# Shifted transposes out of PSUM in 512-column operations, and weight blocks loaded one pair ahead

## The chip, the cores and the metric

One core of a Trainium2 chip runs the whole program in one launch. The time is the device time of that core in microseconds (us). The engines have queues of their own, worked in order: TensorE (PE: matmuls and transposes, results in PSUM), VectorE (DVE), ScalarE (ACT), GpSimd (POOL, which here works on SBUF only) and SyncE (SP), whose queue issues all of this kernel's loads and stores.

## The reference

Two layers of a transformer block on 1024 tokens of width 1024. Each layer has a mixer (differential attention, latent attention and a state-space scan side by side) and an MLP:

```
for l in range(DEPTH):
    mod = (cond @ w_ada[l] + b_ada[l])[:, None, :]
    sh_m, sc_m, g_m, sh_f, sc_f, g_f = jnp.split(mod, 6, axis=-1)
    h = _rmsnorm(x, norm_g[l, 0]) * (1.0 + sc_m) + sh_m
    y = _hybrid_mixer(h, ...)
    x = x + g_m * _rmsnorm(y, norm_g[l, 1])
    h = _rmsnorm(x, norm_g[l, 2]) * (1.0 + sc_f) + sh_f
    y = jnp.square(jax.nn.relu(h @ w_up[l])) @ w_down[l]
    x = x + g_f * _rmsnorm(y, norm_g[l, 3])
```

The change lies where `h` is made (the norm's result, transposed, plus the shift `sh_m` or `sh_f`) and where `h @ w_up` is computed.

## The kernel before

All matmuls work on numbers split in two: `split` makes `hi`, a rounded copy (ACT, L234), and `lo`, the rest (DVE subtraction, L235). `mm3` (L191 to L193) then runs three matmuls for each product: hi by hi, hi by lo, lo by hi.

**The next h.** Tokens are handled in eight tiles of 128. A tile of x is normed by `norm` (ACT square L629 or L631, DVE scaling L632). PE transposes it in eight blocks of 128 columns into PSUM, so that features lie on the partitions. Since the shift belongs to a feature, it is then one number per partition and block. `cut_cols` empties PSUM block by block: ACT writes `hi` with the shift as bias (L638), and DVE writes `lo` from the same block, the shift and `hi` (L639). There are three places:

- `renorm`, in the mixer, makes the MLP's h. Tiles 0 to 3 go through `transp8` with a two-bank PSUM tile (`bank_s`, L648). Tiles 4 to 7 go through `transp_late`.
- `finish`, inside the last group of `mlp_down`, makes the first four tiles of the next layer's h, with `transp8` on one-bank tiles (`bank_t`, two of them, L659).
- `late_norm` makes tiles 4 to 7 of the next layer's h, in the shadow of the next layer's first products.

**The up projection** uses a scheme with seven block products in place of eight (sums and differences of halves). So `transp_late` also makes four combinations of each late tile with the tile four before it, 512 wide each: POOL adds hi and lo of the old tile (L207), DVE combines PSUM, shift and the old tile block by block (L220), two plain subtractions follow (L217), and each result is split. Only then can products of the kind `sums` run. Products of the kind `plain` need the first four tiles alone; `LEAD` = 6 pairs of them run ahead, beside the late tiles (`next(late)`).

The weights of each pair come through `forms`: it takes a staging buffer from an arena, issues the load (L269, 512 KB for a plain block, 1024 KB for a pair), lets POOL make the sums (L277, L278, L280, L283), and hands out split blocks one by one to a ring of four. `queue` holds three blocks ahead of the product that uses them:

```
        parts = self.chain(*(forms(i, True, False) for i in range(LEAD)), *(forms(i, i >= LEAD, True) for i in range(N)))
        queue = [next(parts) for _ in range(3)]
```

So a block's load is issued when the first split of that block is asked for. `mlp_up` adds the products in DVE (L311 to L330), applies relu and square on ACT (L250, L251), and stores the result to DRAM (L252). In the first layer `bg` streams the modulation weights (loads of `w_ada` at L548, DVE products at L563) beside it.

**Order.** The text above gives the order in which instructions are written down. A planner with a cost model then lays them out on each engine: among the instructions that are ready by its own clock, an engine takes the one written first. The order in each queue is fixed when the program is built. The arena hands out the free range that was given back longest ago; a new user of a range waits for the last reader of the old contents.

In `run`, `finish(t)` is called after tile t's last product. It wrote down in this order: the finishing of tile t (`self.finish`: L684, L685, L686, L687), the norm of tile t-2, the transposition of tile t-3. For t = 7 the split of the next layer's first weights (`load_w`, L711 and L712) comes ahead of these.

Of the kernel before, what the change touches and what calls it, by code (L numbers as in the profile page):

```python
# [13 lines left out]
AF = mybir.ActivationFunctionType  # L14
ALU = mybir.AluOpType
AX = mybir.AxisListType

P = 128
# [3 lines left out]
KD = D // P  # L22
DEPTH = 2
FF = 4096
# [8 lines left out]
LEAD = 6  # L33
# [65 lines left out]
def f32(ap):  # L99
    return ap.bitcast(F32)  # L100


def bcast(ap, n):
    return ap.unsqueeze(len(ap.shape)).to_broadcast(list(ap.shape) + [n])


class Net:
# [92 lines left out]
    def transp_late(self, x, hT, t, shift):  # L200

        nc, F = self.nc, self.F
        T = self.sums()
        tok, sl = slice(t * P, t * P + P), slice((t - 4) * P, (t - 3) * P)
        b = [F.get(4, P) for _ in range(2)]
        for n in range(2):
            nc.gpsimd.tensor_add(b[n], *(f32(h[:, n * 4:n * 4 + 4, sl]) for h in hT))  # L207
        ps = self.bank2()
        for k in range(KD):
            nc.tensor.transpose(ps[:, k * P:k * P + P], x[:, k * P:k * P + P], self.ident)  # L210
        pv = ps.rearrange("p (n k q) -> p n k q", n=2, q=P)

        def put(n, a, c, b=None):

            e = F.get(4, P)
            if b is None:
                nc.vector.tensor_sub(e, a, c)  # L217
            else:
                for k in range(4):
                    nc.vector.scalar_tensor_tensor(e[:, k], in0=a[:, k], scalar=b[:, k:k + 1], in1=c[:, k],  # L220
                                                   op0=ALU.add, op1=ALU.subtract)
            self.split(e, *(T[n][:, m, :, sl] for m in range(2)))
            return e

        e1 = put(0, pv[:, 0], b[0], shift[:, 0:4])
        e2 = put(1, pv[:, 1], e1, shift[:, 4:8])
        self.cut_cols(pv[:, 1], shift[:, 4:8], *(h[:, 4:8, tok] for h in hT))
        e3 = put(2, e2, b[0])
        e4 = put(3, b[1], e2)
        F.put(e1, e2, e3, e4, *b)  # L230

    def split(self, src, hi, lo, eng=None):

# [3 lines left out]
    def mlp_up(self, l, hT, bg, late):  # L237
# [3 lines left out]
        nc, F = self.nc, self.F  # L241
# [20 lines left out]
            self.split(src, *r)  # L262
            return r

        def forms(i, plain, sums):

            n = 2 * P if sums else P
            st = F.get(KD, n)
            dma(st, w_up[:, :, i * 2 * P:i * 2 * P + n])  # L269
            a11, a12 = st[:, 0:4, 0:P], st[:, 4:8, 0:P]  # L270
            if plain:
                yield cut(a11)
                yield cut(a12)
            if sums:
                a21, a22 = st[:, 0:4, P:2 * P], st[:, 4:8, P:2 * P]
                s1, s2 = F.get(4, P), F.get(4, P)
                nc.gpsimd.tensor_add(s1, a21, a22)  # L277
                nc.gpsimd.tensor_sub(s2, s1, a11)  # L278
                yield cut(s2)
                nc.gpsimd.tensor_sub(a21, a11, a21)  # L280
                yield cut(a21)
                yield cut(s1)
                nc.gpsimd.tensor_sub(s2, a12, s2)  # L283
                yield cut(s2)
                F.put(s1, s2)
                yield cut(a22)
            F.put(st)

        N = FF // (2 * P)
        parts = self.chain(*(forms(i, True, False) for i in range(LEAD)), *(forms(i, i >= LEAD, True) for i in range(N)))  # L290
        queue = [next(parts) for _ in range(3)]

        def product(b):
# [337 lines left out]
            nc.scalar.activation(junk, x.rearrange("p (a k q) -> p a k q", a=2, q=P), AF.Square, accum_out=ss)  # L631
        nc.vector.scalar_tensor_tensor(xn, in0=x, scalar=self.rstd(ss), in1=a, op0=ALU.mult, op1=ALU.mult)  # L632

    def cut_cols(self, ps, b, hi, lo):

        nc = self.nc
        for k in range(ps.shape[1]):
            nc.scalar.activation(hi[:, k], ps[:, k], AF.Identity, bias=b[:, k:k + 1])  # L638
            nc.vector.scalar_tensor_tensor(lo[:, k], in0=ps[:, k], scalar=b[:, k:k + 1], in1=f32(hi[:, k]),  # L639
                                           op0=ALU.add, op1=ALU.subtract)  # L640

    def transp8(self, x, hi, lo, t, wide=False, b=None):
        nc = self.nc
        sl = slice(t * P, t * P + P)
        if wide:
            ps = self.bank2()
            for k in range(KD):
                nc.tensor.transpose(ps[:, k * P:k * P + P], x[:, k * P:k * P + P], self.ident)  # L648
            pv = ps.rearrange("p (k q) -> p k q", q=P)
            if b is not None:  # L650
                self.cut_cols(pv, b, hi[:, :, sl], lo[:, :, sl])
                return
            nc.scalar.copy(hi[:, :, sl], pv)
            nc.vector.tensor_sub(lo[:, :, sl], pv, f32(hi[:, :, sl]))
            return
# [829 lines left out]
    def run(self, out, dump=None):  # L1485
# [10 lines left out]
        for l in range(DEPTH):  # L1496
# [20 lines left out]
            def finish(t):  # L1517
# [5 lines left out]
                        tail["w"] = list(self.stage_w(I["w_in"][l + 1], self.qk_cols(0), 2))  # L1523
                if more and t == NT - 1:
                    tail["w0"] = self.load_w(tail["w"], 2)
                if t < NT:
                    self.finish(y[t], self.d_x[2 * l], tail["g"], o, t, tail["x"][t % 3], y[t],
                                hT[0][:, :, t * P:t * P + P])
                if more and t > 1:
                    self.norm(tail["x"][(t - 2) % 3], tail["nxt"][0], y[t - 2])  # L1530
                if more and 2 < t < 7:
                    self.transp8(y[t - 3], hT[0], hT[1], t - 3, False, tail["nxt"][1])
                    F.put(y[t - 3])

            bg = iter(())
            if more:
# [50 lines left out]
```

## Time and profile before

| | us |
|---|---|
| median of 3 runs (lowest, highest) | 2843.81 (2833.29, 2847.76) |
| the profiled execution's own time | 2839.2 |
| its span | 2837.3 |
| PE busy | 2642.7 |
| DVE busy | 1746.6 |
| ACT busy | 1134.9 |
| POOL busy | 575.7 |

How to read the lines: a line of the timeline has the start and the length in us, the engine, the line of the kernel, the operation, output and input with their shapes, how many instructions are merged, and in brackets how long the engine was idle before it and what ended that. A line of the waits has who waited for whom, the total, how often, and the longest. In a group of instructions stand the count, the busy time with the mean in ns, and the idle time ahead of them. A line of the stretches has the window, its length, busy time (and instructions) of PE, weight loads, DVE, ACT and POOL, the granted PE clock, the share of the DMA engines and GB/s.

### The profile page before, as it was taken

The page shows a single profiled execution, that of the slowest core. Times are in us where ns is not written, and L with a number is a line of the kernel's source. Part 1 is how long each engine was busy: PE and PEld are TensorE (multiplying, and loading weights), DVE is VectorE, ACT ScalarE, POOL GpSimd, SP SyncE. Part 2 cuts the span into 40 slices and gives each one's busy share as a digit, 9 for nine tenths or more (in the row PEclk, how much of TensorE's full clock was granted, in tenths as well). Part 3 has the DMA queues.
Part 4 walks back from the last instruction along what each step waited for, and adds up shares of the span by engine and source line. Part 5 has one row for each costly group of instructions (what it writes and reads, how often), then busy time and mean ns, then how long its engine had stood idle before and what let it go on. Part 6 is the DMA issues. An engine that isn't in the chain of part 4 may idle for free.

```text
span 2837.3 us, 34952 instructions
## 1 busy us (share of the span) xinstructions
PE 2642.7 (93%) x12530; PEld 2064.6 (73%) x12530; DVE 1746.6 (62%) x3351; ACT 1134.9 (40%) x2265; POOL 575.7 (20%) x509
## 2 busy tenths in 40 slices
PE   5799998999789999999978999998988999999998
PEld 4677776676667777778768777666766888788886
DVE  7767676544867777665583575755448555643435
ACT  5243444544644445121153443345446454631212
POOL 1341244200142220000031113332002532100002
PEclk9899999899899999999998999888999999999999
DMA  6441312313255546543240121123133433532313
GB/s 224 115 136 51 93 59 81 114 55 104 71 170 163 162 142 210 169 148 127 94 150 16 55 85 63 57 78 114 44 119 97 141 115 112 179 134 77 119 44 105
DMA packets 268529, 311.55 MB, mean 110 GB/s; under 512 B 28674, under 2 KB 212164, under 8 KB 268356
## 3 DMA queue, kind: packets, MB, share of 16 engines
q1 hardware_dynamic: 268356, 309.32, 34.2%
q8 instruction: 99, 1.62, 0.2%
q14 instruction: 74, 0.61, 0.1%
HBM read 242.85 MB, written 66.43 MB: 109 GB/s over the span
## 4 chain that ended last, share of the span: by engine, by line
PE 63%; DVE 11%; DMA 8%; issue 2%; ACT 2%; POOL 1%; SPq 0%; DVEq 0%; ACTq 0%; POOLq 0%
PE bank_b L191 10%; PE bank_b L193 9%; PE bank_b L192 9%; PE bank_s L191 8%; PE bank_s L192 8%; PE bank_s L193 8%; PE bank_a L899 2%; PE bank_s L952 2%; DVE split L235 2%; DMA arena_f<-in_w_ada 2%; PE bank_t L912 2%; DVE arena_f L563 2%; DMA arena_f<-in_w_up 1%; DMA d_r<-arena_f 1%; PE bank_b L1046 1%
## 5 line engine op out<-in xcount | busy, mean ns | idle before, releaser
L191 PE MATMUL bank_b<-split 128*128 128x512 f32 (+2 forms) x1824 | 726.5, 399 | 42.2 <-ACT split L234 19.0
L193 PE MATMUL bank_b<-split 128*128 128x512 f32 (+2 forms) x1824 | 708.3, 389 | 6.3 <-DVE split L235 6.2
L192 PE MATMUL bank_b<-split 128*128 128x512 f32 (+2 forms) x1824 | 709.5, 389 | 0.4 <-DVE split L712 0.4
L234 ACT CAST split<-arena_f 128x512 fp32r<-128x512 f32 (+1 forms) x384 | 281.4, 761 | 651.4 <-PE bank_s L192 442.2
L191 PE MATMUL bank_s<-split 128*128 128x512 f32 (+2 forms) x1152 | 456.4, 399 | 23.5 <-ACT arena_f L399 7.9
L192 PE MATMUL bank_s<-split 128*128 128x512 f32 (+2 forms) x1152 | 452.5, 393 | 4.5 <-DVE split L235 1.8
L193 PE MATMUL bank_s<-split 128*128 128x512 f32 (+2 forms) x1152 | 449.7, 390 | 0.0
L191 PEld LDWEIGHTS bank_b<-split 128*128 128x128 f32 x1824 | 353.3, 194 | 122.1 <-ACT split L234 22.5
L235 DVE TENSOR_TENSOR split<-arena_f,split 128x512 fp32r<-128x512 f32 (+1 forms) x384 | 351.7, 934 | 93.6 <-ACT split L234 92.4
L193 PEld LDWEIGHTS bank_b<-split 128*128 128x128 f32 x1824 | 352.1, 193 | 76.2 <-DVE split L235 8.2
L192 PEld LDWEIGHTS bank_b<-split 128*128 128x128 f32 x1824 | 353.6, 194 | 65.3 <-issue 4.7
L401 DVE TENSOR_TENSOR arena_f<-arena_f,bank_s 128x1024 f32<-128x1024 f32 x126 | 153.6, 1219 | 237.5 <-PE bank_s L193 237.4
L191 PEld LDWEIGHTS bank_s<-split 128*128 128x128 f32 (+1 forms) x1152 | 219.3, 191 | 79.3 <-ACT arena_f L399 9.5
L192 PEld LDWEIGHTS bank_s<-split 128*128 128x128 f32 (+1 forms) x1152 | 220.1, 191 | 51.6 <-DVE split L235 3.5
L193 PEld LDWEIGHTS bank_s<-split 128*128 128x128 f32 (+1 forms) x1152 | 219.9, 191 | 44.5 <-issue 0.9
L887 ACT ACTIVATE arena_f<-bank_s,nm 128x128 f32<-128x128 f32 (+4 forms) x192 | 141.9, 741 | 179.9 <-DVE nm L886 157.4
L886 DVE TENSOR_REDUCE nm<-bank_s 128x1 f32<-128x128 f32 (+3 forms) x192 | 142.3, 752 | 114.5 <-PE bank_s L1101 66.9
L563 DVE SCALAR_TENSOR_TENSOR arena_f<-arena_f,cond 128x128 f32<-128x128 f32 x448 | 156.0, 382 | 76.9 <-DMA arena_f<-in_w_ada 42.2
L250 ACT ACTIVATE arena_f<-arena_f 128x512 f32<-128x512 f32 x128 | 80.7, 632 | 138.5 <-DVE arena_f L324 52.2
L915 ACT COPY arena_f<-bank_t 128x512 f32<-128x512 f32 (+1 forms) x160 | 86.6, 541 | 121.0 <-PE bank_t L912 105.8
L952 PE MATMUL bank_s<-split 32*128 32x512 f32 (+3 forms) x576 | 119.2, 378 | 11.1 <-ACT arena_f L887 8.8
L686 POOL TENSOR_TENSOR arena_f<-arena_f 128x1024 f32<-128x1024 f32 x14 | 37.8, 2700 | 445.4 <-DVE rstd_m L183 408.6
(282 smaller groups left out, 3274.1 us busy)
## 6 DMA issues: line engine op xcount, KB each, us to landing
arena_f<-in_w_ada SPq DMA_DIRECT2D x80, 512.0 KB
d_r<-arena_f SPq DMA_DIRECT2D x128, 256.0 KB
arena_f<-in_w_up SPq DMA_DIRECT2D x32, 1024.0 KB
arena_f<-d_r SPq DMA_DIRECT2D x64, 512.0 KB
arena_f<-in_w_down SPq DMA_DIRECT2D x64, 512.0 KB
arena_f<-d_x SPq DMA_DIRECT2D x36, 512.0 KB
d_x<-arena_f SPq DMA_DIRECT2D x23, 512.0 KB
arena_f<-in_w_in SPq DMA_DIRECT2D x20, 512.0 KB
```

The source lines that it names most:

```text
L191: mm(out, wh, xh, start=start, stop=False)
L192: mm(out, wh, xl, start=False, stop=False)
L193: mm(out, wl, xh, start=False, stop=stop)
L234: self.nc.scalar.copy(hi, src)
L235: (eng or self.nc.vector).tensor_sub(lo, src, f32(hi))
L250: nc.scalar.activation(t, t, AF.Relu)
L401: nc.vector.tensor_add(y[t], y[t], ps)
L563: nc.vector.scalar_tensor_tensor(acc, in0=w[:, k], scalar=self.cond[:, k:k + 1], in1=acc, op0=ALU.mult, op1=ALU.add)
L886: nc.vector.tensor_reduce(nm, S[:, 0:n], axis=AX.X, op=ALU.max, negate=True)
L887: nc.scalar.activation(p[:, 0:n], S[:, 0:n], AF.Exp, bias=nm, accum_out=ls)
L915: nc.scalar.copy(held, ps[:, 0:w])
L952: nc.tensor.matmul(S[mp][:, c0:c1], Q[rw, a, tok], K[rw, b, c0:c1], start=a == b, stop=a == 1 and c1 < n)
```

## The change

- `cut_cols` adds the shift to 512 columns of PSUM at once on DVE, into an SBUF buffer `e`, and then splits `e`: ACT copies `hi`, DVE subtracts `lo`. `transp8` with a wide PSUM tile calls it for each half.
- `transp_late` uses the kept `e` (`b22`) for the combinations, and takes the other half of PSUM in one subtraction from `less`, which POOL prepares (old tile less the shift).
- `finish` writes down the transposition of tile t-3 first, then the norm of tile t-2, then the finishing of tile t.
- `mlp_up` issues each w_up load one form earlier (`stage`): the load of form n+1 is issued when form n begins.

```
+        less = F.get(4, P)
+        nc.gpsimd.tensor_sub(less, b11, bcast(shift[:, 0:4], P))
...
-                for k in range(4):
-                    nc.vector.scalar_tensor_tensor(e[:, k], in0=a[:, k], scalar=b[:, k:k + 1], in1=c[:, k],
-                                                   op0=ALU.add, op1=ALU.subtract)
+            nc.vector.tensor_sub(e, a, c)
             self.split(e, *(T[n][:, m, :, sl] for m in range(2)))
             return e
-        e1 = put(0, pv[:, 0], b[0], shift[:, 0:4])
-        e2 = put(1, pv[:, 1], e1, shift[:, 4:8])
-        self.cut_cols(pv[:, 1], shift[:, 4:8], *(h[:, 4:8, tok] for h in hT))
-        e3 = put(2, e2, b[0])
-        e4 = put(3, b[1], e2)
+        b22 = self.cut_cols(pv[:, 1], shift[:, 4:8], *(h[:, 4:8, tok] for h in hT), keep=True)
+        e1 = put(0, less, pv[:, 0], less)
+        e2 = put(1, b22, b22, e1)
+        put(2, b11, e2, b11)
+        put(3, b21, b21, e2)
...
-        def forms(i, plain, sums):
-
-            n = 2 * P if sums else P
-            st = F.get(KD, n)
-            dma(st, w_up[:, :, i * 2 * P:i * 2 * P + n])
+        N = FF // (2 * P)
+        todo = [(i, True, False) for i in range(LEAD)] + [(i, i >= LEAD, True) for i in range(N)]
+        staged = []
+
+        def stage():
+
+            if todo:
+                i, plain, sums = todo.pop(0)
+                st = F.get(KD, 2 * P if sums else P)
+                dma(st, w_up[:, :, i * 2 * P:i * 2 * P + st.shape[2]])
+                staged.append((st, plain, sums))
+
+        def forms():
+
+            stage()
+            st, plain, sums = staged.pop(0)
...
+        stage()
+        parts = self.chain(*(forms() for _ in range(LEAD + N)))
...
-    def cut_cols(self, ps, b, hi, lo):
-
-        nc = self.nc
-        for k in range(ps.shape[1]):
-            nc.scalar.activation(hi[:, k], ps[:, k], AF.Identity, bias=b[:, k:k + 1])
-            nc.vector.scalar_tensor_tensor(lo[:, k], in0=ps[:, k], scalar=b[:, k:k + 1], in1=f32(hi[:, k]),
-                                           op0=ALU.add, op1=ALU.subtract)
+    def cut_cols(self, ps, b, hi, lo, keep=False):
+
+        e = self.F.get(4, P)
+        self.nc.vector.tensor_add(e, ps, bcast(b, P))
+        self.split(e, hi, lo)
+        if keep:
+            return e
+        self.F.put(e)
...
+                if more and 2 < t < 7:
+                    self.transp8(y[t - 3], hT[0], hT[1], t - 3, False, tail["nxt"][1])
+                    F.put(y[t - 3])
+                if more and t > 1:
+                    self.norm(tail["x"][(t - 2) % 3], tail["nxt"][0], y[t - 2])
                 if t < NT:
                     self.finish(y[t], self.d_x[2 * l], tail["g"], o, t, tail["x"][t % 3], y[t],
                                 hT[0][:, :, t * P:t * P + P])
-                if more and t > 1:
-                    self.norm(tail["x"][(t - 2) % 3], tail["nxt"][0], y[t - 2])
-                if more and 2 < t < 7:
-                    self.transp8(y[t - 3], hT[0], hT[1], t - 3, False, tail["nxt"][1])
-                    F.put(y[t - 3])
```

More of the change, by code (lines that the diff above doesn't have):

```diff
@@ L204, in transp_late @@
         tok, sl = slice(t * P, t * P + P), slice((t - 4) * P, (t - 3) * P)
-        b = [F.get(4, P) for _ in range(2)]
-        for n in range(2):
-            nc.gpsimd.tensor_add(b[n], *(f32(h[:, n * 4:n * 4 + 4, sl]) for h in hT))
+        b11, b21 = F.get(4, P), F.get(4, P)
+        for n, b in enumerate((b11, b21)):
+            nc.gpsimd.tensor_add(b, *(f32(h[:, n * 4:n * 4 + 4, sl]) for h in hT))
+        less = F.get(4, P)
+        nc.gpsimd.tensor_sub(less, b11, bcast(shift[:, 0:4], P))
         ps = self.bank2()
@@ L211, in transp_late, with put @@
         pv = ps.rearrange("p (n k q) -> p n k q", n=2, q=P)
[L213 to L218, printed above, removed]
-                for k in range(4):
-                    nc.vector.scalar_tensor_tensor(e[:, k], in0=a[:, k], scalar=b[:, k:k + 1], in1=c[:, k],
-                                                   op0=ALU.add, op1=ALU.subtract)
+        def put(n, e, a, c):
+            nc.vector.tensor_sub(e, a, c)
             self.split(e, *(T[n][:, m, :, sl] for m in range(2)))
             return e
-        e1 = put(0, pv[:, 0], b[0], shift[:, 0:4])
-        e2 = put(1, pv[:, 1], e1, shift[:, 4:8])
-        self.cut_cols(pv[:, 1], shift[:, 4:8], *(h[:, 4:8, tok] for h in hT))
-        e3 = put(2, e2, b[0])
-        e4 = put(3, b[1], e2)
-        F.put(e1, e2, e3, e4, *b)
+        b22 = self.cut_cols(pv[:, 1], shift[:, 4:8], *(h[:, 4:8, tok] for h in hT), keep=True)
[3 more added lines that the diff above has]
+        put(3, b21, b21, e2)
+        F.put(b11, b21, less, b22)
     def split(self, src, hi, lo, eng=None):
@@ L287, in forms @@
             F.put(st)
-        N = FF // (2 * P)
-        parts = self.chain(*(forms(i, True, False) for i in range(LEAD)), *(forms(i, i >= LEAD, True) for i in range(N)))
+        stage()
+        parts = self.chain(*(forms() for _ in range(LEAD + N)))
         queue = [next(parts) for _ in range(3)]
@@ L650, in transp8 @@
             if b is not None:
-                self.cut_cols(pv, b, hi[:, :, sl], lo[:, :, sl])
+                for k0 in (0, 4):
+                    kk = slice(k0, k0 + 4)
+                    self.cut_cols(pv[:, kk], b[:, kk], hi[:, kk, sl], lo[:, kk, sl])
                 return
```

## The prediction, made before the changed kernel was run

> **What bounds the kernel now.** I read the page first, then busy time by stretch, then the timeline of each engine at the three places where TensorE (PE) is not full.
>
> ```profile
> PE 2642.7 (93%) x12530; PEld 2064.6 (73%) x12530; DVE 1746.6 (62%) x3351; ACT 1134.9 (40%) x2265; POOL 575.7 (20%) x509
> PEclk9899999899899999999998999888999999999999
> ...
> core 0: us, PE busy (x) PEld busy (x) DVE busy (x) ACT busy (x) POOL busy (x), PEclk, DMA share, GB/s
> 735.00:800.00 65.00, 46.02 (x189) 35.86 (x188) 50.18 (x105) 33.62 (x69) 16.40 (x13) 0.84 0.27 90
> 820.00:1060.00 240.00, 230.01 (x988) 179.18 (x987) 172.63 (x349) 106.93 (x188) 74.54 (x74) 0.99 0.51 158
> 1465.00:1509.00 44.00, 21.08 (x83) 16.16 (x82) 39.04 (x92) 26.03 (x72) 12.22 (x4) 0.65 0.40 118
> 2165.00:2200.00 35.00, 25.90 (x110) 19.23 (x109) 35.00 (x72) 24.96 (x50) 9.75 (x7) 0.90 0.44 138
> 2220.00:2460.00 240.00, 240.00 (x1061) 198.80 (x1060) 126.09 (x182) 122.83 (x202) 76.24 (x50) 1.00 0.38 126
> ```
>
> PE is busy 93% of the span, so only stretches where it waits can give anything. Three touch the edited code. At 735 to 800 (start of the first MLP, while the last four tiles of h are transposed) PE is idle 65.00 - 46.02 = 19.0 us. At 1465 to 1509 (end of that MLP, next layer's h being made) it is idle 22.9 us and its clock is 0.65. At 2165 to 2200 (second MLP's start) it is idle 9.1 us. DVE is full or nearly so in all three: 50.2 of 65, 39.0 of 44, 35.0 of 35. In the steady part of the MLPs PE lacks 10.0 us in the first and nothing in the second. The ceiling is thus about 61 us of idle time, plus slow-clock time.
>
> **The change part by part.** First the operation counts. The 160 column operations on ACT (L638) and 160 on DVE (L639) become 40 additions out of PSUM (DVE), 40 copies (ACT) and 40 subtractions (DVE), all 512 wide. In the eight late tiles 64 column operations (L220) become 16 subtractions, and POOL gets 8 more (`less`).
>
> ```profile
> L320 DVE TENSOR_TENSOR arena_f<-arena_f,bank_b 128x512 f32<-128x512 f32 x32 | 21.9, 685 | 22.9 <-PE bank_b L193 22.9
> ...
> 753.05 1.90 DVE L220 SCALAR_TENSOR_TENSOR arena_f<-bank_s,arena_f 128x128 f32<-128x128 f32 x7
> 737.89 1.28 DVE L217 TENSOR_TENSOR arena_f<-arena_f 128x512 f32<-128x512 f32 x2
> 761.55 1.66 ACT L234 CAST split<-arena_f 128x512 fp32r<-128x512 f32 x3 [0.66 <-DMA arena_f<-in_w_up]
> 738.71 2.22 POOL L207 TENSOR_TENSOR arena_f<-split 128x512 f32<-128x512 f32 x1 [3.07 <-DVE arena_f L217]
> 739.82 1.66 DVE L235 TENSOR_TENSOR split<-arena_f,split 128x512 fp32r<-128x512 f32 x1
> ```
>
> Seven column operations take 1.90 us back to back and two 512-wide ones 1.28. One alone is 0.34 and 0.68, so a full DVE spends 0.26 on each column operation and 0.60 on each wide one. The wide addition out of PSUM is nearest to L320 (0.685 alone); its second operand is one column spread over 128, which this trace does not show at this width, so I take 0.60 and keep 0.60 to 0.85 as bounds. DVE work over the program: 224 x 0.26 = 58.2 us before, 96 x 0.60 = 57.6 after. **A full DVE gains nothing in throughput.** Only the late tiles gain (12 x 0.26 = 3.1 becomes 4 x 0.60 = 2.4: 0.7 each); the others lose 0.3 each (8 x 0.26 against 4 x 0.60). On ACT 160 operations of about 0.26 become 40 of about 0.52: 21 us less, on an engine that isn't full. What the edit changes is the chain inside one tile.
>
> ```profile
> 1506.37 0.37 ACT L638 ACTIVATE split<-bank_s,arena_f 128x128 fp32r<-128x128 f32 x1 [0.42 <-DVE split L639]
> 1506.77 0.35 DVE L639 SCALAR_TENSOR_TENSOR split<-bank_s,arena_f,split 128x128 fp32r<-128x128 f32 x1 [0.43 <-ACT split L638]
> 1507.15 0.37 ACT L638 ACTIVATE split<-bank_s,arena_f 128x128 fp32r<-128x128 f32 x1 [0.42 <-DVE split L639]
> ...
> 1466.25 1.03 PE L659 MATMUL bank_t<-ident,arena_f 128*128 128x128 f32 x8
> 1484.96 1.97 PE L659 MATMUL bank_t<-ident,arena_f 128*128 128x128 f32 x8 [5.32 <-DVE split L639]
> 1497.07 1.97 PE L659 MATMUL bank_t<-ident,arena_f 128*128 128x128 f32 x8 [4.12 <-DVE split L639]
> 1502.72 0.79 PE L191 MATMUL bank_b<-split 128*128 128x512 f32 x1 [0.38 <-DVE split L639]
> ...
> 1468.89 1.27 DVE L632 SCALAR_TENSOR_TENSOR arena_f<-arena_f,rstd_y 128x1024 f32<-128x1024 f32 x1
> 1484.57 0.60 DVE L639 SCALAR_TENSOR_TENSOR split<-bank_t,arena_f,split 128x128 fp32r<-128x128 f32 x2
> 1534.24 0.60 ACT L768 ACTIVATE split<-bank_b 128x512 fp32r<-128x512 f32 x1 [7.26 <-PE bank_b L193]
> ```
>
> Each ACT operation waits for the DVE operation before it and the reverse, so a column block takes 1507.15 - 1506.37 = 0.78 us and a tile 8 x 0.78 = 6.3, and the PSUM bank is held all that time. After, the bank is free when its addition ends (two halves: 1.3 us), and the tile is split after about 0.68 + 0.62 + 0.68, one half behind the other: 3 to 3.5 us.
>
> **A, the layer boundary.** PE transposes the second tile of the next h at 1466.25, the third only at 1484.96 and the fourth at 1497.07, both waiting for L639, which empties the banks of the tile before. The fourth tile was normed at 1468.89 + 1.27 = 1470.2, so it stood 27 us for a free bank and a place in DVE's queue. The next layer's products begin at 1502.72 when it is split. The edit attacks both causes: banks come free after one operation each, and in `finish(t)` the transposition and the norm are now written ahead of the finishing of tile t, so that the planner gives them DVE first. What is late next: the second half of the tokens. The first half keeps PE busy until 1528.8 (1534.24 less 24 matmuls for the product that L768 empties, at 240.00 / 1061 = 0.226 each in the steady stretch). The last tile's work lies on a DVE that is busy until the stretch's end at 1509, and its own split is 3 us more, so the second half can begin near 1512: at most 1528.8 - 1512, some 17 us. Lower bound: DVE's order stays as it is and only the last ping-pong shrinks, 6.3 - 3 = 3 us; the weight splits in that queue (w_in, L712) are untouched. The tile could be ready by 1485 to 1490 (normed 1470, DVE full, two tiles ahead of it at 2.4 each); I take **12 us**, nearer the upper end because the wait for banks is what the rows name.
>
> **B, start of the first MLP.**
>
> ```profile
> 757.51 0.38 SPq L269 DMA_DIRECT2D arena_f<-in_w_up  x1
> 782.76 2.40 SPq L269 DMA_DIRECT2D arena_f<-in_w_up  x2
> 788.41 1.26 POOL L277 TENSOR_TENSOR arena_f<-arena_f 128x512 f32<-128x512 f32 x1 [17.64 <-DMA arena_f<-in_w_up]
> 768.16 0.80 PE L193 MATMUL bank_b<-split 128*128 128x512 f32 x1 [5.21 <-DVE split L235]
> 773.31 0.40 PE L193 MATMUL bank_b<-split 128*128 128x512 f32 x1
> 776.99 1.03 PE L210 MATMUL bank_s<-ident,arena_f 128*128 128x128 f32 x8
> 791.72 0.79 PE L191 MATMUL bank_b<-split 128*128 128x512 f32 x1 [9.60 <-ACT split L234]
> ...
> SPq L269 <- DVE split L235: 20.3, 2, 15.8
> ```
>
> Both large waits hang on a w_up load. The block issued at 757.51 reaches ACT at 761.55; its DVE split comes late and PE stands 5.21 us. The first whole pair is issued at 782.76, POOL begins its sums at 788.41, PE restarts at 791.72 after 9.60 us. Issuing each block one form ahead moves these loads by one product pair, some 11 us (48 matmuls of 0.226). That covers both waits, if the staging buffer is free: the last row says that L269 itself stood 20.3 us for buffers whose last reader was a split. A block asked for earlier can stand on an older reader, so part of the lead is lost. After each wait PE also runs slowly (0.80 first, 0.40 only from 773.31): 5.1 us at half clock, 2.6 lost. Upper bound 19.0 + 2 x 2.6, but DVE must first finish the late tiles, the last of which is transposed at 776.99 and needs some 8 us of DVE then; with 5 us less standing in front of it and 4 x 0.7 less DVE work I get the sums' operands ready near 780, PE at 780 instead of 791.7. Bounds 0 (buffers never free earlier) to 17. I take **10 us**. The new `less` subtractions stand on POOL, idle for 17.64 us before 788.41, so on POOL they are hidden; their price to DVE is a rival below.
>
> **C, D, E.**
>
> ```profile
> 2194.41 0.79 PE L191 MATMUL bank_b<-split 128*128 128x512 f32 x1 [3.66 <-ACT split L234]
> 2198.11 1.22 PE L191 MATMUL bank_b<-split 128*128 128x512 f32 x2 [2.91 <-ACT split L234]
> 858.75 0.77 PE L191 MATMUL bank_b<-split 128*128 128x512 f32 x1 [3.72 <-DVE arena_f L327]
> ```
>
> C, second MLP's start: two waits of 3.66 and 2.91 behind a DVE that is full, on splits, not on the load. 4 x 0.7 of DVE work falls away: **4 us** of 9.1 with the earlier load, bounds -4 (POOL's price) to 9. D, the steady MLP: an earlier load can save part of 10.0 us in the first and nothing in the second; its longest wait, 3.72, is for DVE, not for w_up: **1 us**, bounds -5 to 5. E, the first four tiles in each mixer: PE has projection products beside them; **1 us**, 0 to 4.
>
> Sum: 12 + 10 + 4 + 1 + 1 = **28 us**. The profiled execution took 2839.2 us, 4.6 under the median of the three runs (2843.8). 2839.2 - 28 = 2811.2, and for the median of the changed kernel 2843.8 - 28 = 2815.8: **2816 us**. Own range from these bounds: gains of 14 to 45, 2799 to 2830.
>
> **The rivals.** *DVE stays the wall.* Throughput is unchanged (58.2 against 57.6), the planner fills the freed places with other work, and PE waits for the next DVE result instead: A 3, B 3, C 1, E 1. About 8 us, 2836, no change. For it: DVE full in all three stretches. Against it: the waits named are for banks and for a load, not for DVE's throughput.
>
> *POOL takes DVE's time.* While POOL adds from 738.71 to 740.93, a DVE split takes 1.66 instead of 0.68: 1 us lost for each such meeting. Late tiles go from 2 POOL additions to 3, and from 6 to 8 DVE operations with both inputs in SBUF (the column operations read PSUM and were not held up). If each added operation meets one, 3 us per tile on eight tiles where DVE is full: 24 us, less what isn't on the path (half): 12, giving 2828, still faster. The Trainium skill, SBUF — State Buffer, section SBUF: two separate sides, says that a GpSimd operation and a DVE one with two SBUF inputs take a shared port in turn for the whole instruction; by that rule every meeting counts, and the trace agrees with the 1.66.
>
> *Slower: the load ahead blocks SP.* SP issues in order. A w_up load asked for one form early and waiting for its buffer holds back the result stores and the w_ada loads behind it. DVE's modulation products wait for w_ada in DVE's own queue, and PE then runs out of banks, as at 858.75: 3.72 us and 2.6 of slow clock, 6.3. 14 pairs of the first MLP run beside w_ada. From 7 pairs hit (44 us) it outweighs the 28 by more than half a percent; at 8 the time is 2843.8 - 28 + 50 = 2866. For it: L269's waits above. Against it: PE lacks just 10.0 us there now.
>
> **How the numbers follow.** A measurement of this kernel can tell about 0.5%, 14 us, from no change. Forecast 0.54 (nearly all of it beyond 14 us), POOL's price 0.11 (mostly faster), DVE the wall 0.22 (same), SP blocked 0.13 (slower). Faster 0.64, same 0.23, slower 0.13. The range has to take in the second and third case and the best bounds: 2794 to 2843; beyond it lie the slower case and the very best, 2 in 10.
>
> **What would show it.** A: the third and fourth tile's transpositions (L659 before) no longer wait some 5 us each, and the next layer's first product starts 10 to 17 us earlier after the MLP's last. B: the first 1024 KB w_up load is issued before PE needs it, and the 9.60 and 5.21 us waits are under 3. C: PE idle under 6 us. Wrong if DVE's splits last 1.6 us far oftener, if SP's waits for buffers grow into the first MLP's steady part, or if the planner moves unrelated work in the second mixer by more than 10 us.

## The result, and the profile after

| | before | changed |
|---|---|---|
| median, us (9 runs each, side by side) | 2841.95 | 2823.61 |
| lowest to highest, us | 2829.83 to 2860.43 | 2815.19 to 2829.68 |
| the profiled execution, us | 2839.2 | 2827.39 |

The ratio is 0.9933, with a 95% interval of 0.9905 to 0.9961: faster by 0.67%, some 19 us, where 28 were forecast. First the busy line and the clock line of the changed kernel's page, then its busy time by stretch; the columns are those of before, and the windows lie at about the same work (the counts in brackets show how far it differs). One of the six executions of the kernel with three buffers further down took 4263.64 us at a granted clock of 0.553, and one of the fastest kernel with the old tail order 2835.25 us; both are left out of ratios and medians.

```profile
PE 2642.5 (94%) x12530; PEld 2066.1 (73%) x12530; DVE 1755.9 (62%) x3223; ACT 1111.0 (39%) x2145; POOL 587.5 (21%) x517
...
PEclk9899988899989999999999998888998999999999
...
core 0: us, PE busy (x) PEld busy (x) DVE busy (x) ACT busy (x) POOL busy (x), PEclk, DMA share, GB/s
750.00:815.00 65.00, 42.10 (x174) 33.12 (x173) 45.32 (x65) 27.21 (x50) 25.67 (x16) 0.79 0.35 113
835.00:1075.00 240.00, 231.92 (x1011) 181.21 (x1010) 184.60 (x369) 108.79 (x192) 68.14 (x70) 1.00 0.50 160
1455.00:1499.00 44.00, 34.31 (x162) 27.95 (x161) 43.91 (x77) 22.40 (x44) 15.16 (x6) 0.92 0.57 176
2157.00:2192.00 35.00, 18.92 (x66) 13.97 (x65) 30.31 (x38) 15.56 (x28) 15.28 (x10) 0.75 0.37 124
```

At the layer boundary (third window) TensorE (PE) does 34.3 us of work in 44 where it did 21.1. At the first MLP's start (first window) it does 42.1 where it did 46.0, and at the second's (last) 18.9 where it did 25.9: two of the three places that were to gain have lost. PE's own rows name the waits:

```profile
1451.52 1.03 PE L669 MATMUL bank_t<-ident,arena_f 128*128 128x128 f32 x8
1457.86 1.04 PE L669 MATMUL bank_t<-ident,arena_f 128*128 128x128 f32 x8
1464.90 1.03 PE L669 MATMUL bank_t<-ident,arena_f 128*128 128x128 f32 x8
1471.69 1.04 PE L669 MATMUL bank_t<-ident,arena_f 128*128 128x128 f32 x8
1480.77 1.05 PE L191 MATMUL bank_b<-split 128*128 128x512 f32 x2
...
804.84 0.79 PE L191 MATMUL bank_b<-split 128*128 128x512 f32 x1 [19.02 <-ACT split L230]
...
2185.60 0.79 PE L191 MATMUL bank_b<-split 128*128 128x512 f32 x1 [7.65 <-ACT split L230]
```

The four transpositions at the boundary follow each other every 7 us and wait for nothing, and the next layer's products start at 1480.77 instead of 1502.72. But the first product of sums in the first MLP now waits 19.02 us where it waited 9.60, and the second MLP's 7.65 where it was 3.66.

To say where time came from I take, in two traces, the start of PE's n-th instruction, and how far the difference moves over a stretch of n. The program is unchanged up to about n = 2830, and the first 620 us differ by up to 16 us between executions all the same, so they are left out. The stretches are: the end of the first mixer with the first tiles of its MLP's h (n 2850 to 3300, in the kernel before 621 to 721 us), the first up projection and the step to the down projection (3300 to 5100, to 1176 us), the boundary (6300 to 6600, 1450 to 1532 us), and the end of the second mixer with the start of its MLP (9300 to 9900, 2080 to 2232 us). One execution stands behind each figure; two executions of the changed program differ by up to 3 us in them. The n of the table is counted in merged rows, which drop about a dozen instructions up to the first of these places and some thirty up to the last; counted singly, as further down where it is said, most figures move by 1 to 2 us, the largest by 3. Where orders differ, n is not exactly the same work. "Order" is the one in which the first three whole loads of w_up (1024 KB) are issued in the first MLP, by pair, where it was made visible.

| kernel | order | first tiles | first up projection | boundary | second start | ratio to before (95%) |
|---|---|---|---|---|---|---|
| changed | | -7.5 | -3.5 | -14.7 | +3.3 | 0.9933 (0.9905, 0.9961) |
| changed, loads named | 1, 2, 0 | -6.1 | -0.7 | -14.1 | +2.2 | 0.9932 (0.9905, 0.9959) |
| old tail order | | -7.4 | -1.4 | -11.9 | -0.2 | 0.9933 (0.9908, 0.9959) |
| old narrow operations | | -2.5 | -16.9 | -0.4 | +14.3 | 0.9967 (0.9946, 0.9987) |
| load ahead alone | 0, 1, 2 | -0.6 | -15.6 | -1.4 | +9.8 | 0.9929 (0.9901, 0.9958) |
| tail order alone | | -0.8 | -1.1 | -2.7 | +2.1 | 0.9976 (0.9956, 0.9997) |
| `less` on DVE | 1, 0, 2 | -4.6 | -11.3 | -13.1 | +8.6 | 0.9924 (0.9898, 0.9951) |
| late tiles as before | 2, 0, 1 | -5.3 | -1.2 | -18.8 | +4.0 | 0.9920 (0.9895, 0.9944) |
| three buffers | 0, 1, 2 | -7.4 | +2.7 | -18.1 | +7.3 | 0.9890 (0.9861, 0.9919) |
| three buffers, `less` on DVE | 0, 1, 2 | -5.8 | -0.1 | -14.4 | +4.2 | 0.9879 (0.9850, 0.9908) |
| three buffers, late tiles as before | 0, 1, 2 | -7.2 | -8.0 | -17.7 | +3.2 | 0.9857 (0.9824, 0.9891) |
| the same, old tail order | 0, 1, 2 | -6.1 | -9.4 | -10.2 | +4.8 | 0.9856 (0.9821, 0.9890) |
| the same, loads swapped | 1, 2, 0 | -6.6 | +8.9 | -14.9 | +0.1 | 0.9914 (0.9884, 0.9943) |

(The last row has the new tail order.)

### The profile page after: what moved, and what is told of

It reads as the page before. It is cut to its first block, busy times and chain, and to the rows that moved or that the text cites. A ratio compares the mean times of both kernels' runs of the same rounds, so it can differ in the third digit from the quotient of the medians.

```text
span 2825.7 us, 34756 instructions
## 1 busy us (share of the span) xinstructions
PE 2642.5 (94%) x12530; PEld 2066.1 (73%) x12530; DVE 1755.9 (62%) x3223; ACT 1111.0 (39%) x2145; POOL 587.5 (21%) x517
## 4 chain that ended last, share of the span: by engine, by line
PE 65%; DVE 11%; DMA 7%; issue 2%; ACT 2%; POOL 1%; SPq 0%; DVEq 0%; ACTq 0%; POOLq 0%
PE bank_b L191 9%; PE bank_b L193 9%; PE bank_b L192 9%; PE bank_s L191 8%; PE bank_s L192 8%; PE bank_s L193 8%; PE bank_s L962 3%; DVE split L231 2%; PE bank_a L909 2%; PE bank_t L922 2%; DVE arena_f L570 2%; DMA arena_f<-in_w_ada 1%; DMA d_r<-arena_f 1%; PE bank_s L656 1%; PE bank_a L938 1%
## 5 line engine op out<-in xcount | busy, mean ns | idle before, releaser
L230 ACT CAST split<-arena_f 128x512 fp32r<-128x512 f32 (+1 forms) x424 | 305.8, 747 | 678.3 <-PE bank_s L192 425.8
L231 DVE TENSOR_TENSOR split<-arena_f,split 128x512 fp32r<-128x512 f32 (+1 forms) x424 | 381.7, 919 | 92.8 <-ACT split L230 92.0
L897 ACT ACTIVATE arena_f<-bank_s,nm 128x128 f32<-128x128 f32 (+3 forms) x192 | 141.8, 740 | 191.8 <-DVE nm L896 160.8
L570 DVE SCALAR_TENSOR_TENSOR arena_f<-arena_f,cond 128x128 f32<-128x128 f32 x448 | 161.7, 387 | 71.4 <-DMA arena_f<-in_b_ada 32.9
```

The costliest lines, as they stand in the source:

```text
L230: self.nc.scalar.copy(hi, src)
L231: (eng or self.nc.vector).tensor_sub(lo, src, f32(hi))
L570: nc.vector.scalar_tensor_tensor(acc, in0=w[:, k], scalar=self.cond[:, k:k + 1], in1=acc, op0=ALU.mult, op1=ALU.add)
L897: nc.scalar.activation(p[:, 0:n], S[:, 0:n], AF.Exp, bias=nm, accum_out=ls)
```

## The experiments

**The loads by name.** The load of each of the first pairs gets a line of its own (L274, L276, L278 for pairs 0, 1, 2).

```
+                if not sums:
+                    dma(st, src)
+                elif i == 0:
+                    dma(st, src)
...
```

> The changed kernel with the loads of w_up for pairs 0, 1, 2 and the rest written on lines of their own; nothing else differs. Theory 1 (the load of pair 0 lost its place): in the first MLP the 1024 KB loads come in the order pair 1, pair 2, pair 0, because pair 0's buffer comes free last; the sums of pair 0 are then POOL's third set, and TensorE's longest wait of the first sums products (19.02 us in the changed kernel) ends right behind them. Rival (the late tiles or the DVE are what TensorE waits for): the loads stand in order 0, 1, 2 and the wait has another cause. Time by both: that of the changed kernel, 2823 us within 8; ratio to before 0.993.

SP's, POOL's, ACT's and PE's rows of this kernel:

```profile
775.83 0.38 SPq L276 DMA_DIRECT2D arena_f<-in_w_up  x1
...
782.26 0.38 SPq L278 DMA_DIRECT2D arena_f<-in_w_up  x1
782.70 0.57 SPq L274 DMA_DIRECT2D arena_f<-in_w_up  x1
...
781.68 1.44 POOL L294 TENSOR_TENSOR arena_f<-arena_f 128x512 f32<-128x512 f32 x1 [16.35 <-DMA arena_f<-in_w_up]
787.69 1.26 POOL L294 TENSOR_TENSOR arena_f<-arena_f 128x512 f32<-128x512 f32 x1 [1.68 <-DMA arena_f<-in_w_up]
791.47 1.26 POOL L294 TENSOR_TENSOR arena_f<-arena_f 128x512 f32<-128x512 f32 x1
...
792.76 0.62 ACT L230 CAST split<-arena_f 128x512 fp32r<-128x512 f32 x1 [11.32 <-POOL arena_f L294]
...
794.78 0.80 PE L191 MATMUL bank_b<-split 128*128 128x512 f32 x1 [18.98 <-ACT split L230]
```

Pair 1 is loaded at 775.83, pair 2 at 782.26, and pair 0, whose products come first, at 782.70. POOL sums three pairs in a row (L294 at 781.68, 787.69, 791.47), ACT splits only what the third gives, and PE starts 2 us after that split begins. Theory 1 holds for what the wait consists of, but no row shows that pair 0's buffer came free last: its load waits for nothing of its own and stands in SP's queue behind pair 2's, which waited 4.8 us for a store of `d_r` to finish with its buffer. The time is that of the changed kernel (2823.71 us).

The text of the change writes a load ahead; the order of the built program does not follow from that. If the buffer is taken a form ahead and the load is left where it was written before, the built program is the same, instruction for instruction on every engine. What the edit changes is which range of the arena a load gets, and so what it waits for.

**Three fixed buffers.** The loads use three buffers in turn, so that their order is that of the pairs.

```
+        bufs = [F.get(KD, 2 * P) for _ in range(NB)]
-                st = F.get(KD, 2 * P if sums else P)
+                st = bufs[turns[0] % NB][:, :, 0:2 * P if sums else P]
+                turns[0] += 1
```

> The changed kernel with three fixed buffers for the w_up loads, taken in turn, so that the loads keep the order of the pairs. Theory 1: pair 0 is summed first; its first form is ready some 3 sums operations (1.3 us each) and two cuts (0.6 + 0.7 us) after its load, so that TensorE's 19 us wait at the first sums products falls to 8 to 12 us, and the kernel is 7 to 11 us under the changed one: 2813 to 2817 us, ratio to before 0.990. Rival 1 (the loads as such are too late on the queue of SP, behind the stores of the rows): the wait falls by less than 3 us, 2821 to 2826 us. Rival 2 (three buffers are too few in the steady MLP): new TensorE waits of over 2 us each from 830 us on, 2830 us or more.

Median 2813.46 us, in theory 1's range. The trace bears its reasoning out in part: pair 0 is loaded at 746.66 and summed on POOL from 755.63 on, and the wait at the first sums is gone; but PE waits 18.28 us ahead of that, at a product of the kind `plain`. After the rows of pair 0, each row of the chain waits for the next or stands behind it; the last four are POOL's queue:

```profile
746.66 0.38 SPq L277 DMA_DIRECT2D arena_f<-in_w_up  x1
755.63 1.74 POOL L297 TENSOR_TENSOR arena_f<-arena_f 128x512 f32<-128x512 f32 x1
...
777.94 0.80 PE L191 MATMUL bank_b<-split 128*128 128x512 f32 x1 [18.28 <-ACT arena_f L328]
777.30 0.59 ACT L328 COPY arena_f<-bank_b 128x512 f32<-128x512 f32 x1
774.07 1.34 ACT L230 CAST split<-arena_f 128x512 fp32r<-128x512 f32 x2 [7.41 <-DVE arena_f L217]
773.34 0.69 DVE L217 TENSOR_TENSOR arena_f<-bank_s,arena_f 128x512 f32<-128x512 f32 x1 [4.59 <-POOL arena_f L209]
...
768.17 1.71 POOL L297 TENSOR_TENSOR arena_f<-arena_f 128x512 f32<-128x512 f32 x1
769.83 1.26 POOL L207 TENSOR_TENSOR arena_f<-split 128x512 f32<-128x512 f32 x1
771.05 1.26 POOL L300 TENSOR_TENSOR arena_f<-arena_f 128x512 f32<-128x512 f32 x1
772.27 1.04 POOL L209 TENSOR_TENSOR arena_f<-arena_f 128x512 f32<-128x512 f32 x1
```

PE needs a bank; the copy that empties it stands on ACT behind the splits of a late tile; that tile waits on DVE for `less` (L209); and on POOL `less` stands behind the sums of the pairs, L297 and L300. So a second theory: the late tiles' new form, above all its new operation on POOL, holds the start. Rival 2 has something too: from 815 to 1055 us, in the steady part, PE is busy 220.08 of 240 us, where it was 231.92 in the changed kernel; the waits named are for DVE, the longest 2.8 us. Whether this kernel is faster than the changed one stays open: the intervals overlap, and its one trace shows the first up projection 3 to 6 us longer.

**The tail in its old order.** finish, norm, transposition as before; the rest as in the change.

```
+                if t < NT:
+                    self.finish(...)
                 if more and t > 1:
                     self.norm(...)
-                if t < NT:
-                    self.finish(...)
...
```

> The changed kernel with the order of the tail of the MLP as before (finish of tile t first, then norm of t-2, then transposition of t-3); wide operations and loads as in the change. Theory 1 (the order makes the gain at the layer boundary): the transpositions of the next layer's first four tiles again wait for their norm, the stretch from the MLP's last products to the next layer's first is 12 to 17 us longer than in the changed kernel, 2836 to 2840 us. Rival (shorter operations on DVE make it): under a third of it comes back, 2824 to 2829 us.

Median 2828.07 us, ratio as the changed kernel's. The boundary keeps 11.9 of 14.7 us. The rival is right: the order is worth about 3 us there, and nothing that the ratio shows.

**The operations in their old width.** `cut_cols`, `transp8` and `transp_late` as before; loads and tail as in the change.

```
-        self.nc.vector.tensor_add(e, ps, bcast(b, P))
-        self.split(e, hi, lo)
+        for k in range(ps.shape[1]):
+            nc.scalar.activation(hi[:, k], ps[:, k], AF.Identity, bias=b[:, k:k + 1])
...
```

> The changed kernel with the operations of 128 columns as before (ACT with bias and DVE with scalar, eight of each for a tile, in transposed and late tiles); loads and order of the tail as in the change. Theory 1 (the order of the tail makes the gain at the layer boundary, the wide operations the gains in the mixers' first tiles): boundary gain of 10 to 15 us kept, the 5 to 6 us at each mixer's first late tiles lost, 2832 to 2836 us. Rival (wide operations carry the boundary too): the boundary loses 10 us or more of its gain, 2840 us or more.

Median 2831.8 us. The boundary gains 0.4 us, and the last of its four transpositions waits again for the bank, as it did before:

```profile
1479.90 0.48 PE L670 MATMUL bank_t<-ident,arena_f 128*128 128x128 f32 x1 [4.00 <-DVE split L650]
```

So the rival's cause is right, the wide operations carry the boundary. Its time is too long, since the first up projection is 13 to 16 us shorter with narrow operations than in the changed kernel. Neither theory had that. With the first tiles counted in, it is 8 to 13 us; this is where the gain of the load ahead had gone.

**`less` on VectorE.** One word in the changed kernel.

```
-        nc.gpsimd.tensor_sub(less, b11, bcast(shift[:, 0:4], P))
+        nc.vector.tensor_sub(less, b11, bcast(shift[:, 0:4], P))
```

> The changed kernel with the one new difference of each late tile (first half of the summed tokens less the shift) on VectorE instead of POOL; loads named by pair. Theory 2 (POOL is what the first MLP's start waits for: its new operation stands among the late tiles' sums and the pairs' sums): TensorE's 19 us wait at the first sums products falls by 5 us or more, 2814 to 2819 us. Rival (what counts is that pair 0 is loaded after pair 1): here pair 0 is loaded second in the first MLP, so the wait falls by one load and one set of sums, some 4 to 6 us, and ends again right behind pair 0's set; without any of both VectorE's extra 0.7 us for each of eight tiles shows alone, 2824 to 2828 us.

Median 2822.42 us. The loads changed places too: pair 1 (L276), then pair 0 (L274).

```profile
766.78 0.38 SPq L276 DMA_DIRECT2D arena_f<-in_w_up  x1
780.26 0.38 SPq L274 DMA_DIRECT2D arena_f<-in_w_up  x1
...
789.36 0.80 PE L191 MATMUL bank_b<-split 128*128 128x512 f32 x1 [13.82 <-ACT split L230]
```

The wait is 13.82 instead of 19.02 us, as the rival had it for a pair 0 that comes second, and the first up projection is 8 to 11 us shorter. The second start gave 5 to 6 of that back (3 when every instruction is counted). The time lies between the two ranges.

**Late tiles as before.** `transp_late` is the old one, the first four tiles stay wide.

```
-        b22 = self.cut_cols(pv[:, 1], shift[:, 4:8], *(h[:, 4:8, tok] for h in hT), keep=True)
-        e1 = put(0, less, pv[:, 0], less)
...
+        e1 = put(0, pv[:, 0], b[0], shift[:, 0:4])
+        e2 = put(1, pv[:, 1], e1, shift[:, 4:8])
...
```

> The changed kernel with the late tiles as before (no new difference on POOL, operations of 128 columns for their first two sums and their split); the first four tiles' transpositions stay wide, loads and tail order as in the change. Theory 2 (the late tiles' new form costs the first MLP its start): the start of the first MLP comes out 10 to 20 us faster than in the changed kernel, as in the kernel with all operations narrow, and the boundary keeps its 12 to 15 us: 2806 to 2814 us, ratio 0.987 to 0.990. Rival (the boundary's gain is the late tiles' too, or it is the order of the pairs' loads alone, which is pair 2, 0, 1 here): 2820 us or more.

Median 2818.3 us: between the two. The boundary keeps its gain (18.8 us), so it doesn't need the late tiles' new form. The start doesn't recover: with the order 2, 0, 1 PE waits 15.84 us at the first sums. The late tiles' form is thus not enough to explain the loss.

**Both: late tiles as before, three buffers.** The two edits above together.

> The kernel of the run before with the three fixed buffers for the w_up loads, so that the pairs are loaded in their order. Theory 1 (the order of the loads) and 2 (the late tiles) together: no TensorE wait over 6 us at the first sums products, 2802 to 2810 us. Rival (three buffers cost the steady MLP what they give at its start, 10 us or so as the trace of the kernel with them shows): 2814 to 2822 us.

Median 2799.68 us, below both ranges, ratio 0.9857: the fastest kernel here, 1.4% faster than before. One wait of 8.47 us is left ahead of the first sums, where the theory had 6 at most.

**The load ahead alone**, on the kernel before (the `stage` lines of the change, nothing else).

> The kernel before with the load of w_up written a pair ahead, and nothing else of the change. Theory (the load ahead gives the first MLP its 10 us where the late tiles are as before): ratio to before 0.994 to 0.998, the first MLP's start 8 to 14 us shorter, the layer boundary within 2 us of before. Rival (it only takes other buffers, and gains nothing): 0.999 to 1.002.

Median 2820.79 us, ratio 0.9929: as much as the whole change. SP's rows, and the same 65 us of the first MLP's start as in the prediction:

```profile
751.10 0.40 SPq L278 DMA_DIRECT2D arena_f<-in_w_up  x1
...
778.41 0.38 SPq L280 DMA_DIRECT2D arena_f<-in_w_up  x1
...
735.00:800.00 65.00, 59.85 (x260) 47.76 (x259) 57.33 (x115) 40.02 (x80) 26.61 (x20) 0.95 0.46 145
```

Here pair 0 (L278) is loaded first, at 751.10, some 30 us earlier than any whole pair was before, and PE is idle 5.2 us of 65, where it was 19.0. The second MLP has its price: there pair 2 is loaded first, and PE waits 11.90 us at the first sums.

**Three buffers, `less` on VectorE.**

> The changed kernel with the three fixed buffers (pairs loaded in their order) and the new difference of the late tiles on VectorE. Theory 2 as it now stands (with the order mended, the last late tile waits for POOL's new difference, which stands behind the first pairs' sums): TensorE's 18.28 us wait before the first sums falls by 4 to 8 us in the first MLP, and the 14.31 us of the second MLP likewise; the two starts gain 8 to 14 us together, 2801 to 2809 us if the clock is that of the kernel with three buffers. Rival (POOL only moved; VectorE, which now has 0.7 us more for each late tile, is what the last tile waits for): the waits stay within 3 us of 18.28 and 14.31, 2813 to 2820 us.

Median 2808.05 us, in the theory's range, but the waits are the rival's: 17.72 and 13.21 us. So the time came out right for a reason that the rows deny.

```profile
773.04 0.79 PE L191 MATMUL bank_b<-split 128*128 128x512 f32 x1 [17.72 <-ACT arena_f L328]
766.67 1.73 DVE L209 TENSOR_TENSOR arena_f<-arena_f 128x512 f32<-128x512 f32 x1 [2.37 <-POOL arena_f L207]
763.72 1.70 POOL L297 TENSOR_TENSOR arena_f<-arena_f 128x512 f32<-128x512 f32 x1
765.38 1.26 POOL L207 TENSOR_TENSOR arena_f<-split 128x512 f32<-128x512 f32 x1
```

The second theory falls in its narrow form: `less` left POOL, and the late tile waits there for the older sum L207, which stands behind the same L297. What of the late tiles' new form makes this tile late was not taken apart further.

**The fastest kernel with the tail in its old order.**

> The fastest kernel so far (late tiles as before, three fixed buffers) with the order of the MLP's tail as before. Theory (the order of the tail gives the boundary 3 us at most; the wide operations of the first four tiles give the rest): 2800 to 2805 us, the boundary within 4 us of the 17.7 us that the fastest kernel gains there. Rival (the tail's order counts here): 8 us or more of the boundary's gain lost, 2808 us or more.

Median 2806.84 us, ratio 0.9856 against 0.9857. The trace shows the boundary 7.5 us longer, between the two expectations; the ratio shows nothing.

**The tail order alone**, on the kernel before.

> The kernel before with the new order of the MLP's tail and nothing else. Theory: it takes the next layer's tiles first in the writing, but VectorE's operations of 128 columns still hold the banks, so the boundary gains under 3 us, ratio 0.998 to 1.002. Rival: it gains half of the boundary's 12 to 15 us, ratio 0.996 or less; or it moves the buffers and with them the second layer's start, ratio over 1.002.

Ratio 0.9976, the boundary 2.7 us shorter: the theory's mechanism, a little beyond its range.

**The fastest kernel with the loads swapped.** The loads of pairs 1 and 2 are written ahead of pair 0's, which takes the third buffer.

```
+        early = {LEAD - 1: [LEAD + 1, LEAD + 2], LEAD: [LEAD], LEAD + 1: []}
...
+            for m in early.get(n, [n + 1] if n + 1 < LEAD + N else []):
+                st = bufs[(m + (2 if sums else 0)) % NB][:, :, 0:2 * P if sums else P]
```

> The fastest kernel (late tiles as before, three fixed buffers) with one thing put back as the changed kernel has it: the first whole loads of w_up come in the order pair 1, pair 2, pair 0 instead of 0, 1, 2, in both MLPs, at the same places of SP's queue; bytes, buffers and operations are the same. Theory 1 (the order of these loads is what costs the start of the first MLP): TensorE waits 14 to 20 us before the first sums product again, until right behind pair 0's set of sums, the start of the first MLP is 8 to 14 us longer than in the fastest kernel, the second MLP's start longer too, and the time is 2808 to 2822 us, ratio 0.989 to 0.993. Rival (the order only came along; the buffers or the late tiles decide): the wait stays under 10 us and the time within 4 us of the fastest kernel's, 2800 us.

Median 2819.27 us, ratio 0.9914 against 0.9857, 20 us by the medians (the intervals overlap at their very ends, 0.9884 and 0.9891). SP's rows of the fastest kernel (L289 pair 0, L291 pair 1, L293 pair 2), those of the swapped one (L292 pair 1, L294 pair 2, L290 pair 0), whose execution runs 12.8 us later here, and PE's at its first sums:

```profile
746.44 0.38 SPq L289 DMA_DIRECT2D arena_f<-in_w_up  x1
769.25 0.40 SPq L291 DMA_DIRECT2D arena_f<-in_w_up  x1
775.88 0.38 SPq L293 DMA_DIRECT2D arena_f<-in_w_up  x1
...
759.23 0.38 SPq L292 DMA_DIRECT2D arena_f<-in_w_up  x1
782.04 0.40 SPq L294 DMA_DIRECT2D arena_f<-in_w_up  x1
788.52 0.38 SPq L290 DMA_DIRECT2D arena_f<-in_w_up  x1
...
800.96 0.80 PE L191 MATMUL bank_b<-split 128*128 128x512 f32 x1 [5.09 <-ACT split L242]
```

The first up projection takes 16.9 us more (+8.9 against -8.0) with the three loads in another order at the same three places of the queue. PE's instructions stand in the same order in both up to n = 4829; counted singly, 6.3 us are lost up to n = 3612, soon after the first sums begin, and 10.3 up to 4600. The other 7 come at the step to the down projection, where the clock fell too (0.66 from 1110 to 1120 us), and one execution can't tell whether they belong to the swap. So it is shown that the order of these loads costs time at the start. Its size and form are not those expected: the wait at the first sums is 5.09 us, not 14 to 20. The fastest kernel's wait of 8.47 us is there in both. At the second start the swap costs nothing (+0.1 against +3.2).

## Why the prediction was right and wrong

The total (2816 forecast, 2823.61 measured) is nearer than its terms, and that is luck: A came out near its forecast, but the gain forecast for B and C didn't come, and what made up for part of it, D and E, stood in the sum with 1 us each. In the changed kernel's two traces:

**A, the layer boundary: 12 forecast, 14.1 and 14.7 measured.** The mechanism is the one named first, banks held through a ping-pong of 128 columns: without the wide operations the gain is 0.4 us. "The edit attacks both causes" was half wrong: the order of the tail alone gives 2.7 us, and taking it out of the change loses 2 to 3 (7.5 in the fastest kernel).

**B, the start of the first MLP: 10 gained forecast, 8 lost measured** (n 3300 to 3600, +7.8 and +8.5). The step that failed is "issuing each block one form ahead moves these loads by one product pair, some 11 us". The written place moves no load here. The buffer does, and in the changed kernel pair 0's load went out last of three: in the execution whose first 620 us are 2.4 us longer than before's, at 782.70, where the first whole load stood at 782.76 before, and now two other pairs were summed ahead of it. So the loss is not lost work. It is E's gain taken back: PE comes to the first sums earlier and leaves them no earlier, as the last operation ahead of the wait shows, in the kernel before and in the one with named loads (whose sums start at 791.72 and 794.78):

```profile
781.73 0.39 PE L193 MATMUL bank_b<-split 128*128 128x512 f32 x1
```

```profile
774.76 1.04 PE L212 MATMUL bank_s<-ident,arena_f 128*128 128x128 f32 x8
```

Of the two waits that the term counted on, that of 5.21 us shrank (none over 1.84 us is left from 745 to 785 us), that of 9.60 doubled. The prediction had the buffers as a loss of part of the lead, not as a change of order. Counted singly from n = 2862 to 3612, so with the first tiles, the changed kernel differs from before by +0.3 us, with late tiles as before by -1.2, with three buffers by -9.5, with both by -14.1, and with both and the loads swapped by -7.8. So the loads in the order of the pairs are worth 9.8 and 12.9 us there together with the buffers, and 6.3 us alone. With the load ahead alone, whose loads stand in order, the stretch of B gains 14.7 us. So the mechanism is there, and the wide operations undid it, as I read it by moving the buffers; what three buffers give back at the start with the new late tiles, the steady part loses again.

**D and what follows: 1 forecast, 11.3 and 9.2 measured**, counted singly some 5.5 in the steady part and 4 to 6 at the step to the down projection. Part of it is, as I read it, time that B had lost, since other engines ran ahead during the wait; with B fast (load ahead alone) the steady part loses 4.5. The 5.4 us at the step, which the load ahead has by itself, were not looked into.

**C, the second start: 4 gained forecast, 2 to 3 lost in a stretch that also holds the second layer's first tiles.** Counted singly, the changed kernel has gained 7.4 us in those tiles when the window of C begins (n = 9691), and is 2.3 behind when it ends (9800): the place of the term itself loses 10. As in the first layer, PE comes early to the first sums and waits (7.65 us there, 3.66 before). The load ahead alone loses 9.8 in the stretch, the wide operations give most of it back. The term was put on DVE's load. Whether the order of the loads decides here is not shown: the swap cost this place nothing.

**E, first tiles: 1 forecast, 6 to 7.5 in the first layer.** The second layer's give about as much (7.4). "PE has projection products beside them" was wrong: without wide operations 0.6 to 2.5 are left, so 4 to 5 us hang on these. Whether through the banks, as at the boundary, is not shown: PE's longest wait from 690 to 765 us of the kernel before was 3.8 us, for a split (ACT L653).

The rivals: that DVE stays the wall is denied at the boundary, where DVE was busy 43.91 of 44 us and the gain came all the same. (The prediction calls DVE full in all three places; at 50.2 of 65 us in the first it was not.) POOL's `less` does not hold DVE up by the 12 us priced; DVE's splits from 700 to 900 us average 0.795 us, and 0.803 with the loads named, against 0.782. SP was not blocked into a loss either: in the steady part PE lacks 8.1 of 240 us, where it lacked 10.0. The nearest to what happened is the rival in which a load asked for early stands in the wrong place, but it was priced for stores and w_ada behind it, not for the pairs among themselves. The estimate for the wide addition out of PSUM held: one takes 0.683 us on average out of `bank_s`, as L320 did (0.685).

The parts do not add. Alone, the load ahead gives 0.7% and the tail 0.2%; all three parts give 0.7%. Wide operations on top of the other two (0.9967 to 0.9933, intervals that overlap) bring 14 us at the boundary, 4 to 5 at the first tiles and 11 to 12 at the second start, and take 13 to 16 from the first up projection. Wide operations alone were not run. Open is whether load ahead with the new tail (0.9967) is slower than load ahead alone (0.9929), since these intervals overlap too, and why; the traces put 4.5 us at the second start.

## What to carry to other kernels

A load written earlier is not a load issued earlier where a planner and an arena stand between: look in the trace at which load goes out first and whose buffer it takes, and give the loads on which the next products hang buffers of their own. An edit that only changes how many scratch buffers a neighbouring step takes can undo another edit, so parts are to be timed alone and together. A bank that is held through eight small operations is worth more than the operations' sum: emptying it in one wide addition gave 14 us at about the same DVE work (1755.9 us in all, 1746.6 before). And time gained ahead of a wait is kept only if what ends the wait comes earlier too: here the first tiles' 7 us were waited away at the first sums, in both layers.

## What the runs showed of the hardware

TensorE's granted clock fell to half in the midst of work. In the changed kernel's profiled execution (first two rows) PE was busy 5.00 of 5.00 us when the clock went to 0.50, and it stayed there for some 20 us; in the next kernel's execution (third row), the same instructions ran at 1.00.

```profile
355.00:360.00 5.00, 5.00 (x31) 3.70 (x30) 3.71 (x6) 1.78 (x6) 2.17 (x1) 0.89 0.00 0
360.00:365.00 5.00, 5.00 (x24) 4.55 (x23) 4.04 (x12) 2.60 (x6) 1.86 (x2) 0.50 0.00 0
```

```profile
360.00:365.00 5.00, 4.56 (x31) 3.77 (x30) 5.00 (x12) 2.72 (x7) 3.47 (x3) 1.00 0.04 10
```

The Trainium skill, TensorE: Matmul & The Clock Gate, section Part 1: The HAM clock gate (the "warmup" mystery), has the half clock follow an idle window of some 3.4 us. The wait in the first MLP agrees with it (the first product after the 19.02 us of idle takes 0.79 us, the products from 809.51 on 0.39); this drop doesn't: no idle time of that length stands in the trace ahead of it, as far as modelled ends can tell. In this pair of executions it and a second one cost the unchanged first 620 us some 10 us (12.5 us more than before in the one, 2.4 in the other). That is most of a run's spread, and the reason why a change of 19 us is read here by stretches.
